# A conditional block that keeps its data in small tiles and is laid out as unlikely

## The chip, the cores and the metric

The kernel runs on one core of one Trainium2 chip. The metric is the device time of one execution in microseconds (us). The core has five engines that run their own instruction streams and meet at semaphores: PE (matrix products), DVE (elementwise work and reductions), ACT (activations and copies), POOL and SP. Here SP issues nearly all transfers from the main memory; 16 DMA engines carry them out.

## The reference

Two layers over 256 tokens of width 1024. Each layer has a token-mixing part (a projection, two kinds of attention, an output projection, a layer norm) and a mixture of experts, followed by a second layer norm. This case is about the experts:

- A router chooses for each token one of 4 groups and in it two of 8 experts, with a weight for each of the two.
- An expert computes, for its tokens, silu(x W_gate) * (x W_up), scaled by the token's weight, times W_down; W_gate and W_up are 1024x256, W_down is 256x1024. There are 32 experts in a layer.
- Their results are added to 1.414 x and to a gated embedding, and the sum is normalized.

How many tokens an expert gets is known only at run time. All numbers are float32.

## The kernel before

**Places.** SBUF holds an arena of 47 places of 128x1024 elements (class `Arena`, `Held`). The planner is Python code that runs once, ahead of time. A load takes the place that has been free longest; any other tile takes the fifth youngest of the free ones (`take`, with `young` 4); `give` puts a place at the young end. At run time a transfer into a place waits until the last reader of what stood there is done. Beside the arena there are small tiles of 128x512 (`t2`, four buffers).

**Slots.** The experts are ranked. The 12 with the most tokens get 64 slots each and the other 20 get 32. Groups of 128 slots are worked through in turn, 11 in a layer: two large experts or four small ones each. For a group, DVE makes marks (which token has which slot, `marks_of`, line 930, tile `gs`), PE gathers the tokens with them (`gather`: x times marks, a copy by ACT at line 907), `front` multiplies with the gate and up weights, `hidden_act` and `turned` make the hidden rows, `back` multiplies with the down weights, ACT and DVE split the result in two parts (lines 208 and 209), and PE adds these to the tokens' rows (`combine`). The weights of an expert are six loads of 512 KB: four for the front and two for the back. Where the rank decides which expert it is, SP reads its number from a table in SBUF (line 1032) and issues the load (line 1038).

**The order.** In the loop over the groups PE's order is written out by hand: the front of group gi + 1, then the back of group gi, the gather for gi + 2, the additions of group gi, and the embedding's products in some groups. SP issues the loads in the order of the program and runs ahead as far as places are free. With the last group but one SP also loads the two rows of the second layer norm (`wide`, line 382), into arena places.

**The conditional block.** An expert can have more tokens than slots. `cmi` holds the largest excess over all experts. Each engine reads it (line 1207, `values_load`) and at `gi == ifat`, 3, between the front of the fifth group and the back of the fourth, comes `leftover` (line 1191): `tc.If(most > 0)` at line 1192 with two loops over the experts in it, whose body is `rest` (line 1073). For one expert and 128 tokens beyond its slots `rest` makes marks, gathers, loads the six weight pieces, computes the expert and adds the result. It takes arena places for the gathered tokens (`Gathered()`) and, one after the other, for the weights (`Held`). Nothing is moved across the block: what stands ahead of it is issued ahead of it on each engine.

## Time and profile before

| | |
|---|---|
| three runs | 974.13, 977.86 and 978.9 us, median 977.86 |
| profiled execution | 975.37 us |
| its span, first to last instruction | 973.2 us |
| PE busy | 913.9 us, 94% of the span |
| weight loads of PE | 605.7 us (62%), beside the matmuls |
| DVE, ACT, POOL busy | 426.4, 347.7, 33.4 us |
| read from main memory | 278.70 MB, 287 GB/s over the span |
| mean granted clock of PE | 0.984 of full speed |

The profile is of one execution. PEld is PE's weight load, an engine name with a q (PEq, SPq) is that engine's sequencer, which issues instructions, branches and handles semaphores without the engine being busy. A gap is put down to the semaphore event that ended it. The experts' stages lie at about 225 to 480 us (layer 0) and 705 to 965 us (layer 1).

### The profile page before, as it was taken

Reading aid. Unit: us, or ns where it says so; the run is one execution under the profiler, and the core shown is the slowest. Engines: PE = TensorE matmul, PEld = TensorE weight load, DVE = VectorE, ACT = ScalarE, POOL = GpSimd, SP = SyncE. Lnnn points to the kernel's source line nnn. Section 1 sums busy time; section 2 is a strip of 40 time slices with the busy share of each in tenths; the row PEclk is TensorE's granted clock in tenths of the full one; section 3 lists DMA queues with packets and bytes.
Section 4 is the critical chain, followed back from the end, with each engine's and each line's share of the span. In section 5 each row is a group of like instructions: output and inputs, shape, how many; then the busy total and the mean of one; then the engine's idle time right before and its main releaser. Section 6 shows DMA issues by size and latency. Waiting matters only on the chain. (4 is left out here: it accounts for less than half of the span.)

```text
span 973.2 us, 15915 instructions
## 1 busy us (share of the span) xinstructions
PE 913.9 (94%) x5761; PEld 605.7 (62%) x5761; DVE 426.4 (44%) x1066; ACT 347.7 (36%) x704; POOL 33.4 (3%) x36
## 2 busy tenths in 40 slices
PE   8999999999998889999899999999999979889994
PEld 5877777885555466544488767787755536466441
DVE  6796566873121111121468854768622111111223
ACT  6557586522121111111346667765112102111120
POOL 0000000100000000000410000001000000000000
PEclk9999999999999899999999999999999999999998
DMA  8994335777859999895998233456767899989934
GB/s 289 406 413 163 129 109 183 259 256 266 335 216 418 412 419 412 327 415 242 374 418 336 87 131 130 143 200 244 284 240 281 305 416 414 419 357 401 405 136 153
DMA packets 79015, 280.89 MB, mean 289 GB/s; under 512 B 9160, under 2 KB 9928, under 8 KB 78928
## 3 DMA queue, kind: packets, MB, share of 16 engines
q1 hardware_dynamic: 78784, 279.78, 75.0%
q8 instruction: 49, 0.80, 0.3%
q14 instruction: 38, 0.31, 0.1%
q10 hardware_dynamic: 144, 0.00, 0.0%
HBM read 278.70 MB, written 1.05 MB: 287 GB/s over the span
## 5 line engine op out<-in xcount | busy, mean ns | idle before, releaser
L92 PE MATMUL acc<-a,a 128*128 128x512 f32 x1440 | 351.7, 398 | 3.1 <-ACT a L208 2.3
L92 PEld LDWEIGHTS acc<-a,a 128*128 128x128 f32 x1440 | 265.9, 189 | 65.0 <-ACT a L208 3.2
L92 PE MATMUL mm<-a,a 128*32 128x512 f32 (+5 forms) x1776 | 236.8, 542 | 0.0
L208 ACT ACTIVATE a<-a 128x512 fp32r<-128x512 f32 (+1 forms) x247 | 150.7, 631 | 99.7 <-PE acc L92 66.6
L209 DVE TENSOR_TENSOR a<-a,a 128x512 fp32r<-128x512 f32 (+1 forms) x239 | 160.5, 692 | 51.3 <-ACT a L208 50.6
L92 PEld LDWEIGHTS mm<-a,a 128*32 128x32 f32 (+3 forms) x1776 | 111.0, 133 | 102.8 <-issue 91.7
L92 PE MATMUL mm<-a,hT 128*32 128x512 f32 x704 | 94.8, 620 | 13.6 <-PEq L1192 8.4
L92 PEld LDWEIGHTS mm<-gs,a 128*128 128x128 f32 x704 | 80.4, 192 | 17.6 <-PE mm L92 11.7
L92 PE MATMUL mm<-gs,a 128*128 128x128 f32 x704 | 84.7, 278 | 0.0
L1048 ACT ACTIVATE sil<-mm 128x256 f32<-128x256 f32 x22 | 8.4, 383 | 184.9 <-PE mm L92 184.9
L92 PEld LDWEIGHTS mm<-a,hT 128*32 128x32 f32 x704 | 24.6, 114 | 77.9 <-issue 61.3
L1049 DVE SCALAR_TENSOR_TENSOR sil<-sil,wsl,mm 128x256 f32<-128x256 f32 x22 | 10.6, 481 | 133.1 <-ACT sil L1048 132.9
L209 DVE TENSOR_TENSOR t<-mm,t 128x512 fp32r<-128x512 f32 x44 | 30.4, 692 | 72.5 <-ACT t L208 72.5
L208 ACT ACTIVATE t<-mm 128x512 fp32r<-128x512 f32 x44 | 26.3, 597 | 86.3 <-PE mm L92 86.3
L763 DVE TENSOR_TENSOR sil<-sil,mm 128x256 f32<-128x256 f32 x16 | 6.7, 420 | 107.4 <-ACT sil L762 107.4
L92 PE MATMUL acc<-t,sT 128*128 128x512 f32 x176 | 48.4, 410 | 0.0
L907 ACT ACTIVATE a<-mm 128x512 f32<-128x512 f32 x40 | 23.9, 597 | 49.9 <-PE mm L92 49.9
L920 DVE CAST sT<-mm 128x256 fp32r<-128x256 f32 x22 | 9.3, 425 | 69.0 <-PE mm L92 69.0
L92 PEld LDWEIGHTS acc<-t,sT 128*128 128x128 f32 x176 | 31.2, 189 | 9.0 <-issue 2.5
L762 ACT ACTIVATE sil<-mm 128x256 f32<-128x256 f32 x16 | 6.1, 383 | 79.6 <-PE mm L92 79.6
L92 PE MATMUL acc<-t,identr 128*128 128x256 f32 x32 | 12.1, 379 | 21.8 <-ACT t L208 20.6
L548 ACT ACTIVATE t<-mm,mx 128x128 f32<-128x128 f32 (+1 forms) x64 | 26.0, 421 | 10.7 <-DVE mx L545 10.7
(195 smaller groups left out, 646.8 us busy)
## 6 DMA issues: line engine op xcount, KB each, us to landing
a<-ws SPq DMA_DIRECT2D x523, 512.0 KB, 9.2
a<-x_in SPq DMA_DIRECT2D x2, 512.0 KB
out<-a SPq DMA_DIRECT2D x4, 256.0 KB
a<-xT_in SPq DMA_DIRECT2D x3, 256.0 KB
a<-wik SPq DMA_DIRECT2D x2, 288.0 KB
a<-ws SPq DMA_DIRECT2D x2, 256.0 KB
pT<-pT_in SPq DMA_DIRECT2D x2, 256.0 KB, 8.5
a<-wrt SPq DMA_DIRECT2D x2, 144.0 KB
```

Of the source, the lines that this page charges most:

```text
L92: self.last = nc.tensor.matmul(*a, **k)
L208: copied[0] = A.activation(hi, src, AF.Copy)
L209: copied[1] = eng.tensor_tensor(lo, src, hi, op=OP.subtract)
L548: A.activation(e[:, i * nk:(i + 1) * nk], b[:, i * nk:(i + 1) * nk], AF.Exp, bias=mx[:, i:i + 1], accum_out=sums[i])
L762: A.activation(g, b[:, :256], AF.Sigmoid)
L763: V.tensor_tensor(g, g, b[:, 256:], op=OP.mult)
L907: A.activation(xg.half[k4], b.rearrange("p (k s) -> p k s", k=4), AF.Copy)
L920: V.tensor_copy(sT, b[:, :2 * P].rearrange("p (t q) -> p t q", t=TT))
L1048: A.activation(sil, gu[:, :FE], AF.Sigmoid)
L1049: V.scalar_tensor_tensor(sil, sil, wsl, gu[:, :FE], op0=OP.mult, op1=OP.mult)
```

## The change

`rest` takes no place of the arena any more. The gathered tokens come in two halves, each into a small tile of 128x4x128; the halves of the gate and up product follow their half of the gather. Each weight piece of 512 KB becomes two loads of 256 KB into small tiles of 128x512, each used by the products that read it. `gather` now does one half per call, and its callers loop over the halves. The `If` gets `preferred_fallthrough_block=False`, an option that names the side which follows directly in the code.

```diff
-        def gather(gs, xg, halves=(0, 1)):
-            for k4 in halves:
-                b = bank()
...
-                A.activation(xg.half[k4], b.rearrange("p (k s) -> p k s", k=4), AF.Copy)
+        def gather(gs, xg, k4):
+            b = bank()
...
+            A.activation(xg, b.rearrange("p (k s) -> p k s", k=4), AF.Copy)
...
-            gather(gs, first, (0,))
+            gather(gs, first.half[0], 0)
...
-            def weights(j):
-                w = Held([2, 512])
-                nc.sync.dma_start(w.t, ws[l, ds(O_EXP + 6 * er + j, 1)].rearrange("o p n -> (o p) n"))
+            def weights(j, k):
+                w = t2([P, 512])
+                src = ws[l, ds(O_EXP + 6 * er + j, 1), :, k * 512:(k + 1) * 512]
+                nc.sync.dma_start(w, src.rearrange("o p n -> (o p) n"))
                 return w
...
-                xg = Gathered()
-                gather(g1, xg)
                 sT = t2([P, TT, P], F32R)
-                bw = ways(g1, [ce], sT)
                 wsl = wt([P, 1], F32, "wsl", 3)
-                V.tensor_copy(wsl, bw)
+                V.tensor_copy(wsl, ways(g1, [ce], sT))
                 gu = bank()
-                for j in range(4):
-                    w = weights(j)
-                    for k in range(2):
-                        kt = 2 * j + k
-                        PE.matmul(gu, xg.half[kt // 4][:, kt % 4, :], w.v[:, k, :], start=kt == 0, stop=kt == KT - 1)
-                    w.free()
-                xg.free()
+                for k4 in range(2):
+                    xg = t2([P, 4, P])
+                    gather(g1, xg, k4)
+                    for k in range(4):
+                        kt = 4 * k4 + k
+                        PE.matmul(gu, xg[:, k, :], weights(kt // 2, kt % 2), start=kt == 0, stop=kt == KT - 1)
...
                 for f in range(2):
-                    w = weights(4 + f)
                     for h in range(2):
-                        PE.matmul(yp[h], hT[:, f, :], w.v[:, h, :], start=f == 0, stop=f == 1)
-                    w.free()
+                        PE.matmul(yp[h], hT[:, f, :], weights(4 + f, h), start=f == 0, stop=f == 1)
...
-            with tc.If(most > 0):
+            with tc.If(most > 0, preferred_fallthrough_block=False):
```

## Rows read from the trace of the kernel before

**Rows 1.** The page: busy time of the engines, share of the span, instructions.
```profile
PE 913.9 (94%) x5761; PEld 605.7 (62%) x5761; DVE 426.4 (44%) x1066; ACT 347.7 (36%) x704; POOL 33.4 (3%) x36
```

**Rows 2.** Waits of all engines: who for whom, us in total, times, longest.
```profile
PE mm L92 <- PEq L1192: 8.4, 2, 4.4
```

**Rows 3.** Line 1192: duration in ns (least/median/longest), first and last start.
```profile
L1192 SPq COMPARE_BRANCH  x2: 45/49/53, 277.1 to 755.5; - x2
L1192 PEldq COMPARE_BRANCH  x2: 5976/6025/6074, 312.4 to 791.0; - x2
L1192 ACTq COMPARE_BRANCH  x2: 45/45/45, 315.3 to 793.8; - x2
...
L1192 DVEq COMPARE_BRANCH  x2: 63/68/72, 316.3 to 794.8; - x2
...
L1192 PEldq EVENT_SEMAPHORE  x2: 51/51/51, 318.5 to 797.0; - x2
```

**Rows 4.** Time order of PE around the block: start, us, operation, idle before.
```profile
307.49 7.07 PE L92 MATMUL mm<-a,a 128*32 128x512 f32 x64
318.91 6.27 PE L92 MATMUL mm<-a,hT 128*32 128x512 f32 x32 [4.35 <-PEq L1192]
...
338.41 3.62 PE L92 MATMUL mm<-a,hT 128*32 128x512 f32 x32
...
786.23 7.08 PE L92 MATMUL mm<-a,a 128*32 128x512 f32 x64
797.39 5.34 PE L92 MATMUL mm<-a,hT 128*32 128x512 f32 x32 [4.08 <-PEq L1192]
```

**Rows 5.** Stretches: PE, PEld, DVE, ACT, POOL busy, granted clock, DMA share, GB/s.
```profile
318.90:325.10 6.20, 6.19 (x32) 1.55 (x32) 0.85 (x2) 0.60 (x1) 0.00 (x0) 0.57 1.02 406
325.10:345.00 19.90, 19.90 (x175) 12.05 (x172) 4.35 (x11) 4.24 (x8) 0.00 (x0) 1.00 1.03 416
...
797.40:802.70 5.30, 5.30 (x33) 1.54 (x33) 0.83 (x2) 0.60 (x1) 0.00 (x0) 0.68 1.02 412
```

**Rows 6.** A DMA queue in 315.9 to 317.1: packets, MB, share of 16 engines.
```profile
q8 instruction: 1, 0.02, 5.6%
```

**Rows 7.** Time order of PE: an embedding's addition, and fronts of later groups.
```profile
306.15 0.85 PE L92 MATMUL acc<-t,identr 128*128 128x256 f32 x2 [1.38 <-ACT t L208]
...
361.44 8.77 PE L92 MATMUL mm<-a,a 128*32 128x512 f32 x64
...
393.06 7.07 PE L92 MATMUL mm<-a,a 128*32 128x512 f32 x64
```

**Rows 8.** DVE's marks behind the block, and SP's waits (total, times, longest).
```profile
318.63 0.42 DVE L930 TENSOR_TENSOR gs<-iom,posm 128x256 f32<-128x256 f16 x1 [2.57 <-PEq L1192]
...
SPq L1192 <- SPq L1192: 2.4, 3, 1.5
...
SPq L1038 <- PEq L1192: 1.8, 2, 1.5
```

**Rows 9.** Two stretches, columns as in Rows 5, and line 1038's transfers.
```profile
389.00:444.00 55.00, 52.10 (x412) 26.80 (x414) 10.98 (x30) 8.27 (x18) 0.00 (x0) 0.97 0.95 376
444.00:462.00 18.00, 18.00 (x160) 9.26 (x152) 3.87 (x10) 3.45 (x7) 0.00 (x0) 1.00 0.46 186
...
DMA to landing us min/median/max: 3.1/9.4/11.6
```

**Rows 10.** The end of the experts' stage in layer 0: SP, then PE.
```profile
444.16 0.34 SPq L1038 DMA_DIRECT2D a<-ws  x1
461.51 0.57 SPq L382 DMA_DIRECT2D a<-lnv  x2
...
451.80 7.07 PE L92 MATMUL mm<-a,a 128*32 128x512 f32 x64
458.69 3.62 PE L92 MATMUL mm<-a,hT 128*32 128x512 f32 x32
...
473.70 2.76 PE L92 MATMUL mm<-a,hT 128*32 128x512 f32 x18 [0.23 <-DMA a<-ws]
```

## The prediction

> **What bounds the kernel now.** I read the page first: PE is busy 94% of the span, no other engine over 44%, so the time is PE's chain of work plus its few gaps [rows 1]. Then the list of waits, where one entry names the lines of this change: the matmuls wait for PE's own sequencer at line 1192, the `tc.If`, 8.4 us in two times, one per layer [rows 2]. Third, line 1192 by itself: each engine compares and branches once per layer. SP, ACT and DVE take 45 to 72 ns for it, PE 5976 and 6074 ns [rows 3]. No instruction of the block (lines 1073 to 1115) is in the trace: no expert was overfull, the block was skipped in both layers, and all that it costs is the skipping.

> Fourth, PE in order of time around it. In layer 0 the front matmuls of the fifth group end at 307.49 + 7.07 = 314.56, and the back matmuls of the fourth begin only at 318.91; in layer 1 it is 793.31 and 797.39. These back matmuls then take 6.27 and 5.34 us, where the same 32 in the next group take 3.62 [rows 4]. [...]

> Why 6 us: the DMA queue of kind "instruction" that moves 16 KB pieces brings one in 315.9 to 317.1, between the start of PE's branch (312.4) and its end (318.5), while the weight loads keep all 16 engines full (share 1.02 [rows 5, 6]). I read this as PE fetching code that it did not hold, the target behind the block. The body is long on PE: three chunks of 42 products, and a float32 product is two matmuls in the trace, each with a weight load (the front's 8 steps on four strips make 64 [rows 4]). On the other engines the body is short, and their branches cost nothing.

> **The change part by part.**

> *The layout.* If the not-taken side comes next in PE's code, its branch should cost what the other engines' do, 45 to 72 ns [rows 3], issued at 312.4 while queued matmuls run until 314.56, so hidden. What stays is the semaphore step behind the branch (51 ns, on each engine but POOL), which I read as standing in for the updates of the skipped block. From it (318.5) to the first matmul (318.91) 0.4 us pass today [rows 3, 4]. I keep 0.4 us as the remaining gap; the bounds are 0.05 (the step alone) and the whole 4.35. Gap saved: 4.35 - 0.4 = 3.95 in layer 0, 4.08 - 0.4 = 3.7 in layer 1. Back matmuls at the upper level again: 6.27 - 3.62 = 2.65 and 5.34 - 3.62 = 1.7. Sum per layer 6.6 and 5.4, together 12.0 us.

> Does the clock stay up? Elsewhere gaps of 1.38 us ahead of the embedding's adds are followed by slow front matmuls in some groups (8.77 at 361.44) and not in others (7.07 at 393.06) [rows 7]. So shorter gaps than this one sometimes cost 1.7 us. After a shift these may fall otherwise: I take zero, with plus or minus 1.7 us twice as bounds.

> [...]

> *What is late next in that place.* The back needs its weights and hT. SP passed the branch at 277.1 [rows 3] and then issued the loads, some 35 us ahead. DVE's marks for the group after the next wait for PE's semaphore step, at 318.63 [rows 8], and PE's gather that reads them comes after the back. Without the stall that step is over at about 314.7, DVE's own branch at 316.35 is then the later one, marks are ready by about 317.5, and the gather is due at 315.0 + 3.6 = 318.6. The cover is 1 us; if it went, the gather would wait by what is missing.

> *Arena to small tiles.* Nothing of the loads and the gather inside the block runs. What reaches outside is the bookkeeping: the block takes and gives places of the arena. Each take there is the fifth youngest free one and each give goes to the youngest end, so the block only permutes the six youngest free places, those freed by the front just before it. The list keeps its length, later takes go by rank in it, so every later tile falls on a place of the same rank. What goes is a true wait: today the first load into a place of these six waits for PE's step, 1.8 us in two times [rows 8]. The load queue is full around it (1.02, 1.03 [rows 5]), so I give it nothing; bounds 0 and 1.8. The small tiles take over the dependency: the copies of the back's results go through tiles that the block now also fills by DMA. They read PE's results, which come after PE's step anyway. Zero, bounds 0 and the 0.4 us of one more handover per layer.

> *The gather's new signature* issues the same matmuls and copies. Zero.

> *Is the saved time given back?* Behind the skip the load queue is full [rows 5], later it has slack (shares of 0.95, then 0.46 [rows 9]). The last weights before the layer-norm rows are issued at 444.16 [rows 10]. Ahead of it stand two loads for the last back, eight for the back at 458.69 and the sixteen of the front at 451.80. At 1.25 us each (512 KB at 416 GB/s [rows 5]) the front's are issued by 431.6 and, with the longest landing of 11.6 us [rows 9], there by 443.2, 8.6 us early; the back's are there by 453.2 (by 451.0 at the median landing, 9.4), 5.5 to 7.7 us early. PE is to come 6.6 us earlier: at worst 1.1 us of waiting, unless the loads, some of which wait for places that PE frees, also move up. The layer then ends on a real stall: the layer-norm rows need a place that PE frees at 461.5, the last weight loads stand behind them on SP, and the last back still waits for them at 473.7 and ends at 476.5 [rows 10]. But what starts that chain is PE, so it moves as a whole, and layer 1 is built the same. Nothing is given back, bound 1.1 us.

> **The sum.** The profiled execution took 975.4 us, of which the span is 973.2 and 2.2 lie around it. 975.4 - 12.0 = 963.4. The median of the three runs is 977.9, 2.5 us above it, which would give 965.9. I forecast 965.5.

> **The rivals.**

> *The jump moves but stays (slower).* The not-taken side comes next, yet the block stands right behind it, so it ends with an unconditional jump over the body. Then PE does its semaphore step first. If this waits for the earlier matmuls (its counterpart on SP did wait, 2.4 us in three times [rows 8]), the fetch begins after 314.56, not at 312.42. Today 2.1 us of it (2.3 in layer 1) lie under queued matmuls [rows 3, 4]; these come into the open, 4.5 us in both layers, and a longer gap may cost one more slow stretch in each, 0 to 3.4 us. Time 982 to 986. For it: the name of the option promises an order of blocks, not a distant place. Against: no row speaks against it; it weighs less with me because a body that stands behind the last instruction needs no jump at all where it is skipped. It decides at the first PE instruction behind the branch.

> *The option changes nothing that PE sees.* Branch and fetch stay, the block is skipped as before: 974 to 979. For it: on the other engines the layout costs nothing, and there is no sign in the trace of how the compiler places blocks. Against: PE's fetch is of the target, and a distant target explains it. That the 4.35 us are something other than the branch's fetch would end here too.

> *The gain is lost at the loads.* If the last weights of a layer came by the load queue's own pace, the 6.6 us of layer 0 would end in its tail, and in the worst case layer 1's 5.4 too: 965.5 + 6.6 = 972 up to 977. Against it the slack worked out above.

> *SP is held at the block.* The small tiles were last read by the embedding's adds, which end at 307.0 [rows 7]; were SP to wait for that ahead of its branch, the load queue would stand still for some 29 us more, from 278 to 307. Its later slack, 5% of 55 us and 54% of 18 us [rows 9], takes up 12.5 of them; some 16 us a layer stay: 965.5 + 32 = 997.5. Against: the block's arena places were in use until 314.6, and SP went by at 277.1; such waits stand inside the block.

> **How the numbers follow.** Forecast 0.58, jump that stays 0.17, no effect 0.15, lost at the loads 0.07, SP held 0.03. The forecast's own range is 961 to 970: 12.0 us, less 0 to 3 for the gap, the clock and the loads, on a base that varies between 974.1 and 978.9, with a little for the clock falling better. For 8 in 10 the range must take in no effect and the loads as well: 961 to 980, which leaves out the two slower cases. About 0.5% (4.9 us) is what a measurement of this kernel tells from no change. Faster by more: the forecast and half of the lost gain, 0.61. Within: no effect, the other half, and a part of the slower jump whose price starts at 4.5 us, 0.21. Slower: 0.18.

> **What would show it.** Line 1192 in the changed kernel: PE's branch at 45 to 110 ns instead of 6 us, and no gap over 0.5 us between front and back at 314.6 and near 787. The back at 3.6 us and the granted clock at 1.00 there. No load that waits for PE's step. No 16 KB piece fetched between branch and step. The end of layer 0 then comes 6 to 7 us earlier. If a BRANCH of several microseconds stands behind the semaphore step, the first rival holds; if the branch keeps its 6 us, the second; if the gap is gone and the layer's end stands, the third. Wrong altogether: SP idle before 314.

## The result, and the profile after

The changed kernel took 982.92 us (median) against 977.79 us for the kernel before: ratio 1.0055, 95% interval 1.0036 to 1.0074. It is slower by 5.1 us, where 12 us less had been forecast. Three executions in all, 1560.83 us here, 1349.79 us of the kernel before and 1849.75 us of `one_loop`, lie far outside the rest and are left out of the ratios. The profiled execution took 986.64 us (span 984.8), 3.7 us over its own median. It has two stretches at a granted clock of 0.50 that the profiled execution of the kernel before does not have, one early in the program (10.69 to 17.52) and one in the front ahead of the block (311.06 to 314.48); before, the clock was 1.00 in 10.69 to 17.52 and over the whole front. So places are compared below, not whole spans.

The page of the changed kernel: busy time, share and instructions of each engine. PE is still the bound, as in [rows 1].

```profile
PE 920.0 (93%) x5761; PEld 607.8 (62%) x5761; DVE 426.5 (43%) x1066; ACT 348.0 (35%) x704; POOL 33.4 (3%) x36
```

Its list of waits (total, times, longest). The entry of [rows 2], 8.4 us on PE's sequencer, is gone. In its place stands a longer one, again one per layer, put down to "issue": time in which PE waited for nothing that the profile names.

```profile
PE mm L92 <- issue: 13.0, 2, 6.5
```

Line 1187, the `tc.If` of the changed kernel: ns min/median/max, first and last start. First the whole trace, then PE alone in a stretch before and a stretch behind the end of its front matmuls in layer 0.

```profile
L1187 PEldq COMPARE_BRANCH  x4: 81/3022/5992, 317.1 to 800.6; - x4
L1187 ACTq COMPARE_BRANCH  x4: 34/38/39, 320.0 to 801.1; - x4
L1187 PEldq EVENT_SEMAPHORE  x2: 51/51/51, 319.4 to 800.5; - x2
...
L1187 PEldq COMPARE_BRANCH  x1: 98/98/98, 317.1 to 317.1; - x1
...
L1187 PEldq EVENT_SEMAPHORE  x1: 51/51/51, 319.4 to 319.4; - x1
L1187 PEldq COMPARE_BRANCH  x1: 5946/5946/5946, 319.5 to 319.5; - x1
```

Each engine now branches four times, not twice [rows 3]. PE's first branch is cheap, as forecast: 98 ns at 317.1 (81 ns in layer 1). Then comes the semaphore step at 319.4, and behind it a second branch of 5946 ns (5992 in layer 1). The trace does not name a branch's target. In the listing of the built program (not a trace) the second branch is an unconditional jump that stands straight ahead of the block's body and goes to what follows it; in the kernel before the body stands first and the not-taken side behind it.

PE in order of time, both layers: start, us, operation, idle before.

```profile
310.49 8.77 PE L92 MATMUL mm<-a,a 128*32 128x512 f32 x64
325.77 6.48 PE L92 MATMUL mm<-a,hT 128*32 128x512 f32 x32 [6.52 <-issue]
...
793.32 7.07 PE L92 MATMUL mm<-a,a 128*32 128x512 f32 x64
806.91 6.55 PE L92 MATMUL mm<-a,hT 128*32 128x512 f32 x32 [6.51 <-issue]
```

The front ends at 310.49 + 8.77 = 319.26, the step runs at 319.4, the jump from 319.5 to 325.45, the back from 325.77. Nothing of the jump lies under matmuls any more. The gaps were 4.35 and 4.08 us [rows 4] and are 6.52 and 6.51: +2.2 and +2.4, together 4.6. The backs (the down-weight matmuls that follow the gap) took 6.27 and 5.34 us and take 6.48 and 6.55: +1.4 together.

Stretches, columns as in [rows 5]: the gap, the back, and what follows it in layer 0, then the gap and the back in layer 1.

```profile
319.26:325.77 6.51, 0.00 (x0) 0.03 (x1) 1.33 (x3) 0.38 (x1) 0.00 (x0) 0.66 1.03 410
325.77:332.20 6.43, 6.42 (x33) 1.57 (x33) 0.69 (x1) 0.60 (x1) 0.00 (x0) 0.55 1.02 409
332.20:352.00 19.80, 19.80 (x174) 11.97 (x171) 4.35 (x11) 4.24 (x8) 0.00 (x0) 1.00 1.03 417
...
800.39:806.90 6.51, 0.01 (x1) 0.02 (x1) 1.33 (x3) 0.38 (x1) 0.00 (x0) 0.67 1.03 413
806.90:813.40 6.50, 6.49 (x33) 1.56 (x33) 0.69 (x1) 0.60 (x1) 0.00 (x0) 0.54 1.03 417
```

The backs now run at 0.55 and 0.54 of full speed throughout (0.57 and 0.68 before). The gaps themselves lie partly at the lower clock (means of 0.66 and 0.67). The load queue stays full across them (share 1.03).

The queue of kind "instruction", 322.9 to 324.1: packets, MB, share of the 16 engines.

```profile
q8 instruction: 1, 0.02, 5.8%
```

One 16 KB piece (the page has 49 of them with 0.80 MB), as in [rows 6], 3.4 us behind the start of the jump: 319.5 to 322.9 now, 312.4 to 315.9 or 316.0 before.

DVE's marks behind the block, to set beside [rows 8]: start, us, operation, idle before.

```profile
321.81 0.42 DVE L929 TENSOR_TENSOR gs<-iom,posm 128x256 f32<-128x256 f16 x1 [1.05 <-DVEq L1187]
```

They wait for DVE's own step now, not for PE's, and come 4 us ahead of the back: off the path.

The end of layer 0's experts: SP, then PE.

```profile
468.62 0.59 SPq L382 DMA_DIRECT2D a<-lnv  x2
...
480.45 2.76 PE L92 MATMUL mm<-a,hT 128*32 128x512 f32 x18 [0.30 <-DMA a<-ws]
```

Against 461.51 and 473.70 [rows 10] both are 7 us late. That is what was lost up to the block's back: 3.0 us before the front began, 1.7 in the front (8.77 for 7.07), 2.2 in the gap, 0.2 in the back. In this execution later slack takes up none of it.

### The profile page after: what moved, and what is told of

Its sections match the earlier page's. It is cut to its first block, busy times and chain, and to the rows that moved or that the text cites. A ratio compares the mean times of both kernels' runs of the same rounds, so it can differ in the third digit from the quotient of the medians.

```text
span 984.8 us, 15951 instructions
## 1 busy us (share of the span) xinstructions
PE 920.0 (93%) x5761; PEld 607.8 (62%) x5761; DVE 426.5 (43%) x1066; ACT 348.0 (35%) x704; POOL 33.4 (3%) x36
```

## The experiments

The block was skipped in every run, as before, so the time of its own path was never measured; the variants of its body below are judged by the cost of skipping alone.

### The two halves of the change

`flag_only` is the kernel before with the option alone:

```
-            with tc.If(most > 0):
+            with tc.If(most > 0, preferred_fallthrough_block=False):
```

> The kernel before with the option on the If alone; the block keeps its arena places. Theory 1 (the jump moved, it did not go: PE first does its semaphore step, which waits for its own matmuls, and only then jumps over the body, so that the 6 us of fetching no longer begin under queued matmuls): the whole slowdown is the option's, ratio 1.0055 within 1.003 to 1.008, PE gaps of 6.4 to 6.6 us at the block in both layers, two branches on PE, the second of 6 us. Rival (the small tiles are what costs, by waits or by transfers): ratio 1.000 within 0.002, gaps as before, 4.1 to 4.4 us.

`tiles_only` is the changed kernel without the option, that is, with the small tiles and the new signature of the gather:

```
-            with tc.If(most > 0, preferred_fallthrough_block=False):
+            with tc.If(most > 0):
```

> The changed kernel without the option: small tiles in the block, the If as before. Theory 1: ratio 1.000 within 0.002, gaps of 4.1 to 4.4 us, one PE branch of 6 us a layer that begins 2 us before PE's matmuls end; no load waits for PE's semaphore step any more (1.8 us before), which is worth nothing. Rival (the tiles cost): ratio 1.003 to 1.008 with gaps elsewhere, or a PE gap of 6.5 us here too.

The first took 979.02 us, ratio 1.0025 (0.9997 to 1.0054), the second 977.6, ratio 1.0005 (0.998 to 1.0031). PE in time order and its branches, option alone:

```profile
321.61 4.98 PE L92 MATMUL mm<-a,hT 128*32 128x512 f32 x32 [6.61 <-issue]
...
799.71 6.56 PE L92 MATMUL mm<-a,hT 128*32 128x512 f32 x32 [6.51 <-issue]
...
L1192 PEldq COMPARE_BRANCH  x4: 81/3045/6086, 312.9 to 793.4; - x4
```

The same for the tiles alone:

```profile
322.12 5.34 PE L92 MATMUL mm<-a,hT 128*32 128x512 f32 x32 [4.32 <-PEq L1187]
...
L1187 PEldq COMPARE_BRANCH  x2: 6017/6024/6032, 315.7 to 792.0; - x2
```

The option alone makes the second branch and the long gap. The tiles alone leave one branch a layer, the gaps of before (4.32 and 4.12 us) and the time of before. The time of the option alone fell just under the 1.003 to 1.008 that I had expected, and its interval reaches no change.

Both the option and the whole change were timed once more:

> The option alone once more. Gaps of 6.4 to 6.6 us in both layers, ratio 1.003 to 1.006 if the gaps' 4.5 us and a slow stretch or two decide; 1.001 to 1.003 if part of them is given back at the layers' ends.

> The changed kernel once more, beside its parts on the same chip. If the option alone makes the slowdown, this and the option alone are the same, both at 1.003 to 1.006, and the difference seen so far (1.0055 against 1.0025) is spread. If the two edits work together (an extra wait only where tiles and option meet), this stays at 1.004 to 1.007 and the option alone at 1.001 to 1.003.

Option alone 979.7 us, ratio 1.0031 (1.0009 to 1.0053); whole change 981.7, ratio 1.0056 (1.0032 to 1.0081). The difference between them came back, 2 to 3 us, but the intervals overlap.

### Is the time the fetch of a distant target?

`hint` is the kernel before with a hint to PE, ahead of the front, that the branch will be taken:

```
-            with tc.If(most > 0):
+            with tc.If(most > 0, label="skip"):
...
+                with in_turn():
+                    tc.mark_branch_hint_location("skip", hint="LikelyTaken", engines=[mybir.EngineType.PE])
```

> The kernel before with one instruction more on PE: a prefetch hint for the If's jump, likely taken, put ahead of the front that precedes the block, some 6 us ahead of the branch. Theory (the 6 us are the fetch of code that PE does not hold): the 16 KB piece comes before the branch, PE's branch takes under 1 us, the gaps fall from 4.35 and 4.08 to about 0.4 us, the backs behind them run at the upper level (3.6 us instead of 6.3 and 5.3), 12 us less, ratio 0.988 within 0.985 to 0.991. Rival (the stall is the branch's own, or a wait for PE's queue): gaps and ratio as before, 1.000 within 0.002. In between, a hint that starts the fetch but too late: 0.993.

`short_body` has the layout of the kernel before and the small tiles of `tiles_only`, and a shorter body: one loop with one chunk for all experts in place of two loops with three chunks. It leaves out the second chunk of the large experts and starts their first at the wrong slot, so the block would be wrong if it ran.

```
-                with tc.For_i(0, NBIG, 1) as r:
-                    rest(r, 64, 2)
-                with tc.For_i(NBIG, NE, 1) as r:
-                    rest(r, 32, 1)
+                with tc.For_i(0, NE, 1) as r:
+                    rest(r, 32, 1)
```

> Small tiles, no option, and a body a third as long: one loop with one chunk for every expert from slot 32 on. It leaves out the second chunk of the 12 large experts and starts the first at the wrong slot for them; the block does not run here, so this shows only in the code's length. Theory (the fetch of a far target): the target lies about a block of 16 KB closer, in code that PE has fetched in sequence, so that the gap goes to about 0.4 us, ratio 0.988; if a block's edge falls between, it goes in one layer alone, 0.994. Rival (every taken branch of PE costs 6 us, however far): gaps of 4.1 to 4.4 us, ratio 1.000 within 0.002.

`hint` took 970.59 us, ratio 0.9931 (0.9907 to 0.9955), `short_body` 968.31, ratio 0.9902 (0.9868 to 0.9937). Line 1192 and PE in time order, with the hint; then the row of that queue from the page, with the hint and before:

```profile
L1192 PEldq COMPARE_BRANCH  x2: 439/458/478, 312.4 to 790.1; - x2
...
L1192 DVEq EVENT_SEMAPHORE  x2: 21/21/21, 316.8 to 794.4; - x2
...
307.47 7.07 PE L92 MATMUL mm<-a,a 128*32 128x512 f32 x64
317.10 5.11 PE L92 MATMUL mm<-a,hT 128*32 128x512 f32 x32 [2.56 <-DVEq L1192]
...
794.69 5.25 PE L92 MATMUL mm<-a,hT 128*32 128x512 f32 x32 [2.30 <-DVEq L1192]
...
q8 instruction: 47, 0.77, 0.3%
...
q8 instruction: 49, 0.80, 0.3%
```

The branch starts at 312.4 as in [rows 3] and takes 439 and 478 ns, not 5976 and 6074. That is less than the 1.1 us for which a 16 KB piece alone was under way before (5.6% of 16 engines over 1.2 us [rows 6]), so none can lie whole in the branch any more, and the queue brings 47 pieces in all, not 49. With nothing else changed, those 5.5 us go with that piece. That it is the target's code is my reading; no trace names a target. The shorter body, whose target lies nearer, does the same without a hint (330 and 445 ns).

The gap does not fall to the forecast 0.4 us, though. It ends at 2.56 and 2.30 us, with another releaser: DVE's own step of the skipped block, at 316.8. PE's step is over at 314.7, but DVE works on the front's result until 316.05 and takes its branch and its step only then. `short_body` has the same gaps (2.57 and 2.00 us). Here my expectations were wrong too: the hint's gain is 6.1 us by the medians (970.59 against 976.69), not 9 to 15.

### The whole block, short

`one_loop` is the changed kernel without the option, with the body in one loop over 44 pieces of an expert, listed in a small table that the block builds first. It leaves nothing out.

```
+                items = [(0, NBIG, 64.0), (0, NBIG, 192.0), (NBIG, NE, 32.0)]
...
+                    V.tensor_scalar(ov[:, 0, :, c], posm[:, :, f:e], start, None, op0=OP.subtract)
+                    V.tensor_copy(ov[:, 1, :, c], cw[:, :, f:e])
+                    V.tensor_copy(ovi[:, c], ids[:, f:e])
...
+                with tc.For_i(0, ni, 1) as r:
+                    rest(r, ov, ovi)
```

> A complete block with a short body: one loop over 44 pieces (two chunks of each of 12 large experts, one of each of 20 small ones), its tables of ranks, weights and numbers built by DVE inside the block, small tiles, no option, the block in its old place. Theory (fetch by distance): like the incomplete short body, PE's branch under 0.5 us, ratio 0.990 within 0.987 to 0.994, gaps of 2.0 to 2.6 us that end with DVE's semaphore step. Rival (the incomplete one won by what it left out): ratio 1.000, gaps over 4 us.

970.2 us, ratio 0.9926 (0.9897 to 0.9954). PE's branch took 330 and 458 ns, and the wait list has the same second wait as the hint's:

```profile
PE mm L92 <- DVEq L1187: 4.6, 2, 2.6
```

`short_flag` is `one_loop` with the option:

```
-            with tc.If(most > 0):
+            with tc.If(most > 0, preferred_fallthrough_block=False):
```

> The one-loop block in its old place with the option. Theory (the option costs only by moving the start of the far fetch behind the semaphore step): with a target that PE has already fetched the option costs nothing, both PE branches under 0.5 us, gap of 2.0 to 3.0 us as without it, ratio 0.990 to 0.994. Rival (the option's layout costs by itself, by the second branch): gaps 2 us longer than without it, ratio 0.995 to 0.998.

966.87 us, ratio 0.987 (0.9836 to 0.9905). Branches and waits:

```profile
L1187 PEldq COMPARE_BRANCH  x4: 64/194/397, 311.9 to 789.6; - x4
...
PE mm L92 <- DVEq L1187: 4.0, 2, 2.1
```

The same option, the same second branch, and no loss: the second branch is short (397 ns at most). So the option's price here is the fetch behind the step, and it went with the length of the body (jumps of 5946 and 5992 ns over the long one). The ratio came out below the 0.990 to 0.994 that I had expected, but its interval overlaps `one_loop`'s, so it shows no gain by the option.

### The block where nothing of DVE is late

DVE's step is late because the block stands straight behind the front. `moved` puts `one_loop`'s block behind the back, the gather and the additions that follow, and gives its marks a small tile of their own. To do so it also ends the hand-written order of PE at that point, in every group.

```
-            if gi == ifat:
-                leftover(most)
...
+            if gi == ifat:
+                leftover(most)
+            with here():
                 embeds(gi)
```

> The same short and complete block, moved behind the fourth group's back, the gather and the additions, where DVE and ACT are done before PE (its marks then lie in a small tile too). Theory (what is left of the gap is PE waiting for DVE's step, since DVE still works on the hidden rows when PE is done): gap of 0.6 us or less at the block, no slow stretch behind it, 3 to 5 us less than the block in its old place, ratio 0.985 to 0.987. Rival (another engine's step takes its place, ACT's or SP's, or SP now waits at the block for loads in flight and the weights come late): a gap of 1.5 us or more there or waits for weights later, ratio 0.990 or above.

It took 1003.66 us, ratio 1.0283 (1.0242 to 1.0323): a miss by far. SP's and PE's rows around the block, and one of SP's waits (total, times, longest):

```profile
315.54 1.29 SPq L164 DMA_DIRECT2D a<-ws  x3
...
L1187 SPq COMPARE_BRANCH  x2: 45/49/53, 316.9 to 811.3; - x2
...
321.72 0.41 PE L95 MATMUL mm<-identr,gs 128*128 128x128 f32 x2 [0.36 <-PEq L1187]
...
326.71 1.88 PE L92 MATMUL mm<-a,a 128*32 128x512 f32 x2 [4.24 <-DMA a<-ws]
...
SPq L164 <- PE mm L92: 63.1, 5, 29.6
```

PE's gap at the block is indeed 0.36 us. But three loads of the next embedding (line 164), whose places PE frees late, now stand ahead of SP's branch. Line 164 waits for PE's matmuls 63.1 us in all, where it was 4.4 us in the kernel before. SP waits with these loads until 315.5 and passes the branch at 316.9, where it used to pass at 277.1 [rows 3]; the next loads of weights go out at 323.49, and PE waits 4.24 us for weights. This is the prediction's rival "SP is held at the block", by another dependency.

`moved_in_order` ties these three loads behind the loads of their own group:

```
+            fetching[0] = nc.sync.dma_start(fetched[r, j].t, src)
...
-                    emb[q] = Embed(q)
+                    with behind(fetching[0]):
+                        emb[q] = Embed(q)
```

> The moved block again, with the three loads of the next embedding (they had slipped ahead of SP's branch and held it, waiting for places) tied behind the loads of their own group. Theory: SP passes the branch before 300 us again, no wait for weights behind the block, the gap at the block about 0.4 us (it was 0.36 in the run before) and no slow stretch behind it; ratio 0.985 to 0.988, 3 to 5 us under the one loop in its old place. Rival (the block there costs by something else as well): 0.990 or above.

954.4 us, ratio 0.9756 (0.9724 to 0.9787), the best of all. SP, PE and DVE at the block, and PE in time order:

```profile
L1188 SPq COMPARE_BRANCH  x2: 45/49/53, 284.2 to 751.7; - x2
...
L1188 DVEq EVENT_SEMAPHORE  x2: 21/21/21, 315.7 to 782.4; - x2
L1188 PEldq COMPARE_BRANCH  x2: 236/288/339, 317.1 to 784.1; - x2
...
319.90 0.41 PE L95 MATMUL mm<-identr,gs 128*128 128x128 f32 x2 [0.30 <-PEq L1188]
...
320.58 7.07 PE L92 MATMUL mm<-a,a 128*32 128x512 f32 x64
327.48 3.62 PE L92 MATMUL mm<-a,hT 128*32 128x512 f32 x32
```

SP passes at 284.2, DVE's step (315.7) comes before PE's branch (317.1), the gap is 0.30 us, and the matmuls behind it take 7.07 and 3.62 us, as at a clock of 1.00 before (307.49 to 314.56 and 338.41 to 342.03). The gain was larger than the expected 0.985 to 0.988, so two runs took it apart. `split_only` leaves `one_loop`'s block in its place and only ends the hand-written order ahead of the embedding's products; `moved_kept` moves the block, with the loads tied, and keeps that order in all other groups.

```
                     sT = after[1]
+            with here():
                 embeds(gi)
```

> The one-loop block in its old place; of the moved kernel only its side effect, the written order of PE ends ahead of the embedding's products, so that the planner issues seven products of the first embedding some groups earlier. If the moved kernel's unexpected part (2.4% where 1.3 to 1.5% were expected) comes from these products, this is 0.982 to 0.986, its first addition of the embedding has no gap of 1.38 us, and the gaps at the block are the one loop's 2.0 to 2.6 us. If it comes from the place of the block, this is the one loop's 0.990 to 0.993.

```
+                if gi == ifat:
+                    one.close()
+                    leftover(most)
+                    one.enter_context(here())
                 embeds(gi)
```

> The moved block with the loads in order, and the written order of PE kept in all groups but the one with the block, so that the seven products stay where they were. What the place alone is worth: 0.984 to 0.988 if the DVE wait and the slow stretch behind it are all (4 us in layer 0, 3 in layer 1, under the one loop's 0.990 to 0.993), gap at the block 0.3 to 0.4 us. If the place carries the whole unexpected part: 0.975 to 0.979.

`split_only`: 960.96 us, ratio 0.9832 (0.9803 to 0.986). `moved_kept`: 963.22, ratio 0.9858 (0.9822 to 0.9894). From `one_loop`'s 0.9926 the split is worth 0.9% and the move 0.7%; both together 1.6%, and `moved_in_order` has 1.7%. Each ratio has an interval of about 0.3% to either side, so the two parts are rough. The split is no matter of the block: it lets some products of an embedding go earlier. Two entries of the wait lists, `one_loop`:

```profile
PE acc L92 <- ACT t L208: 20.6, 15, 1.4
...
PE mm L95 <- DVE sil L1050: 2.8, 2, 1.4
```

and `split_only`, where the second one is gone:

```profile
PE acc L92 <- ACT t L208: 17.9, 13, 1.4
```

That is 5.5 us of the 9 us between the two; the rest of the split's gain is not traced to a place.

### Where the time lies, over all runs

Each run has a span and a mean granted clock. (1 - clock) x span is what the lower clock would take away if PE worked all the time and at a pace that goes with the clock, as it roughly did in the backs (3.62 us at 1.00, 6.27 at 0.57, 6.48 at 0.55); clock x span is the rest. Means over each kernel's runs, in us:

```
                       (1 - clock) x span   the rest
before                 17.0 to 18.6         957.3 to 957.8
tiles_only             16.8                 958.0
flag_only, flag_again  18.4, 17.9           959.1, 959.6
after, changed_again   20.9, 20.1           960.1
hint                   13.4                 955.0
one_loop               13.3                 954.2
short_flag             10.2                 954.1
moved_in_order         10.5                 942.1
```

The first column is not all loss, because it also counts time in which PE stood idle at the lower clock. The gap of layer 0 before (columns as above; the one in layer 1 ran at full speed):

```profile
314.60:318.90 4.30, 0.00 (x0) 0.02 (x1) 1.17 (x3) 0.38 (x1) 0.00 (x0) 0.83 1.03 416
```

The two gaps at the block hold 0.17 x 4.30 = 0.7 us of this column before. In the trace of the change they hold 0.34 x 6.51 + 0.33 x 6.51 = 4.4 us (3.0 in `changed_again`), and with the option alone 4.2 us (`flag_only`, clock 0.69 and 0.67 in its gaps). If these executions stand for the means, the rest of the column is about 17 us before (17.3 - 0.7), 16 to 17 after the change (20.5 less 4.4 or 3.0) and 14 with the option alone (18.2 - 4.2). This is an estimate. By it the change's extra time is about the longer gaps (4.6 us), with no more lost in PE's work than before. With the option alone a part of the slow stretch falls into the longer gap instead of on matmuls, which fits that gaps longer by 4.7 us cost only 2 to 3 us.

What the whole change loses beyond the option, 2 to 3 us, shows in the traces for the most part in the backs: 13.0 us in two layers and again 12.8 (`changed_again`), against 11.5 and 10.0 with the option alone (`flag_only`, `flag_again`). The gaps of the two are the same (6.4 to 6.6 us). Why the backs differ stays open; the tiles alone, without the option, have 11.6 us.

## Why the prediction was wrong

**The step that failed** is the first: "If the not-taken side comes next in PE's code, its branch should cost what the other engines' do, 45 to 72 ns [rows 3], issued at 312.4 while queued matmuls run until 314.56, so hidden. What stays is the semaphore step". The first half held: 98 and 81 ns, hidden under the front (the signs allowed up to 110 ns, a figure that no row and no run shows). The second did not: behind the step stands a jump over the body, with the same fetch as before (5946 and 5992 ns), so the gaps grew to 6.5 us where 0.4 us had been forecast. The rival "The jump moves but stays" had it right in mechanism, in place (behind the semaphore step) and in the price of the gaps: 4.5 us in the open, 4.6 measured. Its 0 to 3.4 us for slow stretches were 1.4 us in the backs of the profiled execution. That the time, 982.9 us, lies in its 982 to 986 is in part luck: with the option alone the gaps grew as much and the time by only 2 to 3 us. I set this rival at 0.17 on the thought that "a body that stands behind the last instruction needs no jump at all". No row said where the body stood. Without a row for "far away", that rival deserved as much as the forecast.

**Why the step waits until the front has ended.** The prediction put this under the rival as an "if", with its counterpart on SP as the sign [rows 8]. It is so: branch at 317.1, front's end at 319.26, step at 319.4. With the option alone it is 312.9, 315.00 and 315.1, and with the hint 312.4, 314.54 and 314.6. In the kernel before the fetch came first and the step after it, so 2.1 us of fetch were free; the new order took this cover away.

**The 0.4 us of residual gap** failed too, where it could be seen. With the fetch gone (`hint`), 2.56 and 2.30 us stay. I had put DVE's branch at 316.35 as the next late thing, but only for the marks and the gather; the back itself waits for DVE's step. With the hint the two gaps gave 3.6 us where the prediction's gap term had 7.65 (3.95 + 3.7), and in the profile the backs gave 1.25 (6.27 to 5.11 and 5.34 to 5.25) where 4.35 stood. So even with the jump gone, an estimate by the hint's places is some 5 us, not 12. The whole times of the four kernels without the far fetch (`hint`, `short_body`, `one_loop`, `short_flag`) lie 6 to 11 us under the kernel before by the medians, so the sum was wrong in its terms by more than in its total. Why the back needs DVE's step (perhaps a tile that the block too would have written) was not tried. The upper level of the sum is in the traces a granted clock of 1.00, at which a back takes 3.62 us; the lowest clock seen over a stretch is 0.50 (311.06 to 314.48 after the change).

**Right were:** that the 6 us go with a piece of code that is fetched (`hint`, `short_body`). In the kernel before and in the changed one a 16 KB piece lies inside each branch of 6 us, in both layers: 315.9 to 317.1 and 794.5 to 796 in the old one, 322.9 to 324.1 and 803.8 to 805.3 in the new jump. The branches of 0.2 to 0.5 us are shorter than the 1.0 to 1.1 us of one piece. Further, that the arena's places, the load that waited for PE's step (that wait is no longer in the list) and the gather's signature are worth nothing that can be measured (`tiles_only`, 1.0005). And that nothing is given back at the loads: in the profiled execution the 7 us of delay reach the end of layer 0 whole.

## What to carry to other kernels

Laying out a block as unlikely did not remove the jump here, it moved it behind the semaphore step. Ask which instruction passes over the body, how far it must go, and what the engine must have finished before that instruction: here that decided how much of the fetch was hidden (2.1 and 2.3 us before, nothing after the change). A shorter body or a hint ahead of the branch took the wait for the fetch away in these runs (branches of 0.3 to 0.5 us for 6 us). Then the next engine's step of the skipped block was late, so put the block where all engines that it names have little outstanding (a gap of 0.30 us in `moved_in_order`). When a block is moved in the order, look first at what each DMA-issuing engine now has ahead of its branch (three loads held SP until 315.5 in `moved`).
